# A decoder layer's products, from column-major to token-major

## The chip, the cores and the metric

The kernel runs on one core of one Trainium2 chip. The metric is the device time of one execution in microseconds (us); several executions are timed and their median is given. PE is the matrix engine, PEld its weight loads, DVE the vector engine, ACT the scalar engine, POOL GpSimd, SP the engine whose queue issues most DMAs. For a matmul the *stationary* operand (128 x up to 128) is loaded first, and the columns of the *moving* operand (up to 512) stream against it.

## The reference

One layer over 256 tokens of 2048 channels, float32. Three sub-layers, each with an RMS norm in front and a residual sum behind:

```python
h = h + 0.5 * swiglu(rms_norm(h, g1), w_gate1, w_up1, w_down1)      # 2048 -> 5632 -> 2048
proj = rms_norm(h, gm) @ w_in        # q, k, v of 16 forgetting heads, gates; q, k, v of window heads
o = concat([rms_norm(o_fox, gf), rms_norm(o_swa, gs)])
h = h + o @ w_out
h = h + 0.5 * swiglu(rms_norm(h, g2), w_gate2, w_up2, w_down2)
# swiglu(x) = (silu(x @ w_gate) * (x @ w_up)) @ w_down
```

## The kernel before

All large products are made with float32 operands cut into two parts, `hi` and `lo`, that add up to the value; of the four partial products the smallest is left out. Weights come in blocks of 1024 columns in all (512 KB): the SP queue loads `raw`, ACT copies it to `whi` (L93), DVE makes the rest `wlo` (L94). Each of these tiles has four buffers, and a block's three steps are queued with high priority, ahead of the work that stands near them in the program.

Activations are kept channel by channel: `h` holds 16 row tiles of 128 channels by 256 tokens, and `u` holds, for each row tile, the hi and lo parts side by side, 512 columns. In the feed-forward halves and the output projection (`column_major`, `columns`, L202 and L203) a 128 x 128 piece of weights is stationary: `whi` against the 512 columns of `u` (both parts), and `wlo` against the 256 columns of the hi part. The result is a 128-channel tile of [hi part | lo part] which `halves_sum` adds up (L225 on ACT, L226 on DVE). In `gated` the token's scale 1/rms, broadcast over all partitions by `rstd_rows` (L183 on PE), is multiplied in on DVE (L234), ACT takes the SiLU (L235), DVE the product (L236), and ACT and DVE cut the result into the tile `hT` (L238, L239), which the down product reads as its moving operand. `into` makes the next stage's `u` from finished rows of `h` (L150, L151) and sums squares on POOL (L163); `rstd_tokens` sums those over partitions on PE (L170).

The mixer's input projections are already made the other way round (`token_major`, `mm3`, L189 to L191): a 128 x 128 piece of `u` is stationary, and 512 (or 388) columns of weights stream, three products for each of two token tiles. The heads are then handled four at a time (`softmax_pv`): scores into PSUM tiles tagged `sc`, soft-max, PE transposes of the probabilities (L454), products with the values. PSUM's eight banks are two accumulators of two banks, two `sm` tiles and two `sc` tiles.

The output projection takes the window half first, then the forgetting half. POOL multiplies its result by the token scale and adds it to `h` (L681, L682). The first feed-forward half begins with both accumulators of its first block at once, in pieces that follow the loads of x; the last down block finishes its two column halves one after the other, so that the first store goes out earlier.

The program is unrolled. Each engine works through its own queue in order, and the order is written by a planner: among instructions whose operands its own clock takes to be ready, the one that stands earliest in the program goes first, so that later products fill gaps in the attention.

Of the kernel before, what the change touches and what calls it, by code (L numbers as in the profile page):

```python
# [17 lines left out]
P = 128  # L18
D = 2048
# [12 lines left out]
CW = 256  # L32
NCH = FF // CW
NEG = -3.0e38

# columns of the constants and of the packed vectors
# [32 lines left out]
def hybrid_layer(ctx: ExitStack, tc: tile.TileContext, a: dict, out: bass.AP):  # L69
# [6 lines left out]
    def acc_tile():  # L76
        return ps.tile([P, 2, 512], F32, tag="acc", name="acc", bufs=2)

    def small_ps(tag="sm"):
        return ps.tile([P, 512], F32, tag=tag, name=tag, bufs=2)  # L80

    # ---------------------------------------------------------------- weights
# [18 lines left out]
    h = keep.tile([P, KD, SEQ], F32, name="h")  # L101
# [63 lines left out]
    def rstd_tokens(ssq, width, tag):  # L165
        """[P, NT], the tokens' 1 / rms, from sums of squares by partition."""
# [9 lines left out]
    def rstd_rows(ssq, width, tag):  # L176
        """[P, SEQ], the same in every partition."""
        r = rstd_tokens(ssq, width, tag + "t")
        dg = sp.tile([P, NT, P], F32, tag="dg", name="dg")
        pb = small_ps()  # L180
        for t in range(NT):
            nc.vector.tensor_scalar_mul(dg[:, t, :], ident, r[:, t : t + 1])
            nc.tensor.matmul(pb[:, t * P : (t + 1) * P], lhsT=ones, rhs=dg[:, t, :], start=True, stop=True)  # L183
        rows = sp.tile([P, SEQ], F32, tag=tag, name=tag)
        nc.scalar.copy(rows, pb[:, :SEQ])
        return rows

# [5 lines left out]
    # ------------------------------------------------------- feed-forward half  # L193
    def banks(acc):
        return acc[:, 0, :], acc[:, 1, :]

    def column_major(acc, w, u, k0, k, last, cols=(0, 1)):
        """acc[j] += (128 x 256 weights).T @ parts of u; its halves' sum is the product."""
        hi, lo = w
        for j in cols:  # L200
            s = slice(k0 * CW + j * P, k0 * CW + (j + 1) * P)
            nc.tensor.matmul(acc[j], lhsT=hi[:, s], rhs=u(k), start=(k == 0), stop=False)  # L202
            nc.tensor.matmul(  # L203
                acc[j][:, 0:SEQ], lhsT=lo[:, s], rhs=u(k)[:, 0, :], start=False, stop=(k == last - 1)
            )

    def columns(acc, src, nk, u, apart=0):
        """acc = the products of nk row tiles; the columns' halves one after the other in the last ones."""
        late = []
        for b in range(nk // 4):  # L210
            with tc.high_priority():
                parts = weights(src[b])
            for k in range(4 * b, 4 * b + 4):
                if k < nk - apart:
                    column_major(acc, parts, u, k % 4, k, nk)
                else:
                    late.append((parts, k))
        for j in range(2):
            for parts, k in late:
                column_major(acc, parts, u, k % 4, k, nk, (j,))  # L220

    def halves_sum(pool, acc, tag):
        n = acc.shape[1]
        t = pool.tile([P, 2, SEQ], F32, tag=tag, name="t", bufs=1 if tag == "tu" else 2)[:, :n, :]
        nc.scalar.copy(t, acc[:, :, SEQ:])  # L225
        nc.vector.tensor_tensor(out=t, in0=acc[:, :, 0:SEQ], in1=t, op=ALU.add)  # L226
        return t

    def gated(pool, acc, rb, hT, c):
        rbb = rb.unsqueeze(1).broadcast_to([P, 2, SEQ])  # L230
        v = {}
        for nm in ("g", "u"):
            v[nm] = halves_sum(pool, acc[nm], "t" + nm)
            nc.vector.tensor_tensor(out=v[nm], in0=v[nm], in1=rbb, op=ALU.mult)  # L234
        nc.scalar.activation(v["g"], v["g"], AF.Silu)  # L235
        nc.vector.tensor_tensor(out=v["u"], in0=v["u"], in1=v["g"], op=ALU.mult)  # L236
        hs = hT[:, 2 * c : 2 * c + 2, :, :]
        nc.scalar.copy(hs[:, :, 0, :], v["u"])  # L238
        nc.vector.tensor_tensor(  # L239
            out=hs[:, :, 1, :], in0=v["u"], in1=hs[:, :, 0, :].bitcast(F32), op=ALU.subtract  # L240
        )

    def gate_up(pool, u, rb, hT, wg, wu, c0=0):
        for c in range(c0, NCH):
            acc = {}
            for nm, w in (("g", wg), ("u", wu)):
                acc[nm] = acc_tile()
                columns(banks(acc[nm]), w[c], KD, u)
            gated(pool, acc, rb, hT, c)

    def down(pool, hT, w, done, last_apart):
        for c in range(KD // 2):
            hc = h[:, 2 * c : 2 * c + 2, :]
            if not (last_apart and c == KD // 2 - 1):
                acc = acc_tile()
                columns(banks(acc), w[c], KF, tiles_of(hT))
                ends = [(acc, hc)]
            else:
                acc = [small_ps(), small_ps()]
                columns(acc, w[c], KF, tiles_of(hT), 8)  # L260
                ends = [(acc[j].unsqueeze(1), hc[:, j : j + 1, :]) for j in range(2)]
            for i, (part, hp) in enumerate(ends):
                t = halves_sum(pool, part, "tg")
                nc.vector.scalar_tensor_tensor(out=hp, in0=t, scalar=0.5, in1=hp, op0=ALU.mult, op1=ALU.add)
                done(2 * c + i, hp)

    def into(u, ssq, gcol):
        """Of two row tiles of h that are finished: the parts for u, and the squares."""

        def done(k0, hc):  # L270
            for k in (k0, k0 + 1):
                split_scaled(u(k), h[:, k, :], vec[:, gcol + k : gcol + k + 1])
            add_squares(ssq, hc, k0 == 0)

        return done

    def token_major(acc, u, nk, src_w, width=512):
        """acc[:, t, :width] = u.T @ weights, for both token tiles."""
        for kg in range(nk // 2):
            with tc.high_priority():  # L280
                hi, lo = weights(src_w[kg])
            for k in range(2):
                kk = kg * 2 + k
                m = slice(k * width, (k + 1) * width)
                for t in range(NT):
                    ts_ = slice(t * P, (t + 1) * P)
                    mm3(
                        acc[:, t, :width], u(kk)[:, 0, ts_], u(kk)[:, 1, ts_], hi[:, m], lo[:, m],
                        start=(kk == 0), stop=(kk == nk - 1),
                    )  # L290

    # ------------------------------------------------------------ first FFN
# [3 lines left out]
    with tc.tile_pool(name="f1", bufs=1) as fp:  # L296
        hT = fp.tile([P, KF, 2, SEQ], F32R, name="hT1")
        # the tensor engine's clock rises while it works: products of zeros until the first operands come
# [5 lines left out]
        take = into(u1, ss1, V_G1)  # L304
        acc = {"g": acc_tile(), "u": acc_tile()}
        tiles = {}

        def piece(nm, c):
            if c % 2 == 0:
                tiles[nm] = weight_tiles()  # L310
            at = c % 2 * 512
            weights(a["w%s1" % nm][0][c // 2][:, at : at + 512], tiles[nm], at)
            for k in range(2):
                column_major(banks(acc[nm]), tiles[nm][1:], u1, c % 2 * 2 + k, 2 * c + k, KD)

        for c in range(10):
            if c < 8:
                hc = h[:, 2 * c : 2 * c + 2, :]
                nc.sync.dma_start(hc, a["xT"][c])
                take(2 * c, hc)  # L320
                piece("g", c)
            if c >= 2:
# [441 lines left out]
```

## Time and profile before

| | |
|---|---|
| runs | 1848.87, 1857.62, 1866.74 us; median 1857.62 us |
| profiled execution | span 1855.6 us from the first to the last instruction, 26310 instructions (the page gives no other time for it) |
| PE, PEld | busy 1842.8 us (99%), 1604.5 us (86%), 10428 instructions each |
| DVE, ACT, POOL | busy 1142.0 us (62%), 895.5 us (48%), 91.1 us (5%) |
| DMA | 337.99 MB, mean 182 GB/s |
| PE's granted clock | 1.000 |

Busy time of an engine is the union of its instructions' durations. A matmul's duration includes the time in which its results travel through the array, which overlaps the next matmul; a rate is read from the distance between starts. A windows row counts each instruction that touches the window.

### The profile page before, as it was taken

Reading aid. Unit: us, or ns where it says so; the run is one execution under the profiler, and the core shown is the slowest. Engines: PE = TensorE matmul, PEld = TensorE weight load, DVE = VectorE, ACT = ScalarE, POOL = GpSimd, SP = SyncE. Lnnn points to the kernel's source line nnn. Section 1 sums busy time; section 2 is a strip of 40 time slices with the busy share of each in tenths; the row PEclk is TensorE's granted clock in tenths of the full one; section 3 lists DMA queues with packets and bytes.
Section 4 is the critical chain, followed back from the end, with each engine's and each line's share of the span. In section 5 each row is a group of like instructions: output and inputs, shape, how many; then the busy total and the mean of one; then the engine's idle time right before and its main releaser. Section 6 shows DMA issues by size and latency. Waiting matters only on the chain.

```text
span 1855.6 us, 26310 instructions
## 1 busy us (share of the span) xinstructions
PE 1842.8 (99%) x10428; PEld 1604.5 (86%) x10428; DVE 1142.0 (62%) x1394; ACT 895.5 (48%) x1182; POOL 91.1 (5%) x73
## 2 busy tenths in 40 slices
PE   8999999999999999999999999999999999999999
PEld 6888888888888888998888888888888888888887
DVE  8556665655655555658767797566666666544443
ACT  6444444444444444455766655444444444443432
POOL 2000000000000000000001462000000000000000
PEclk9999999999999999999999999999999999999999
DMA  7666555665555565565345356666665655666663
GB/s 254 190 188 187 184 190 183 187 187 184 191 184 191 185 189 185 170 203 173 115 147 159 114 161 188 188 191 193 190 186 192 193 187 190 192 189 202 191 200 114
DMA packets 97211, 337.99 MB, mean 182 GB/s; under 512 B 10816, under 2 KB 12992, under 8 KB 97088
## 3 DMA queue, kind: packets, MB, share of 16 engines
q1 hardware_dynamic: 94752, 334.10, 57.4%
q10 hardware_dynamic: 2336, 2.21, 0.3%
q8 instruction: 82, 1.34, 0.3%
q14 instruction: 41, 0.34, 0.0%
HBM read 334.17 MB, written 2.10 MB: 181 GB/s over the span
## 4 chain that ended last, share of the span: by engine, by line
PE 97%; DVE 2%; issue 1%; ACT 1%; DMA 0%; DVEq 0%
PE acc L202 53%; PE acc L203 28%; PE acc L189 4%; PE acc L191 4%; PE acc L190 4%; DVE wlo L94 1%; PE sm L202 1%; PE sm L203 1%; PE sc L558 1%; PE sm L454 1%; PE sm L460 1%; PE sc L630 1%; DVE u L151 0%; PE sm L609 0%; PE sm L461 0%
## 5 line engine op out<-in xcount | busy, mean ns | idle before, releaser
L94 DVE TENSOR_TENSOR wlo<-raw,whi 128x1024 fp32r<-128x1024 f32 (+2 forms) x648 | 794.8, 1229 | 667.8 <-ACT whi L93 667.5
L93 ACT CAST whi<-raw 128x1024 fp32r<-128x1024 f32 (+2 forms) x648 | 665.7, 1029 | 897.0 <-PE acc L202 629.6
L202 PE MATMUL acc<-u,whi 128*128 128x512 f32 x2944 | 1033.2, 395 | 1.7 <-DVE t L226 1.0
L203 PE MATMUL acc<-u,wlo 128*128 128x256 f32 x2944 | 826.9, 281 | 4.2 <-DVE wlo L94 4.2
L202 PEld LDWEIGHTS acc<-u,whi 128*128 128x128 f32 x2944 | 551.9, 188 | 132.1 <-DVE t L226 1.3
L203 PEld LDWEIGHTS acc<-u,wlo 128*128 128x128 f32 x2944 | 556.2, 189 | 7.8 <-DVE wlo L94 7.0
L202 PE MATMUL acc<-hT,whi 128*128 128x512 f32 x1320 | 463.5, 393 | 0.0
L203 PE MATMUL acc<-hT,wlo 128*128 128x256 f32 x1320 | 373.3, 283 | 0.0
L202 PEld LDWEIGHTS acc<-hT,whi 128*128 128x128 f32 x1320 | 247.9, 188 | 57.3
L203 PEld LDWEIGHTS acc<-hT,wlo 128*128 128x128 f32 x1320 | 248.2, 188 | 0.0
L189 PE MATMUL acc<-whi,u 128*128 128x512 f32 (+1 forms) x320 | 120.1, 375 | 0.6 <-ACT pr L583 0.6
L191 PE MATMUL acc<-whi,u 128*128 128x512 f32 (+1 forms) x320 | 119.4, 373 | 0.0
L190 PE MATMUL acc<-wlo,u 128*128 128x512 f32 (+1 forms) x320 | 119.4, 373 | 0.0
L226 DVE TENSOR_TENSOR t<-acc,t 128x512 f32<-128x512 f32 x119 | 81.2, 682 | 0.0
L225 ACT COPY t<-acc 128x512 f32<-128x512 f32 x119 | 68.9, 579 | 0.7 <-PE acc L203 0.7
L189 PEld LDWEIGHTS acc<-whi,u 128*128 128x128 f32 x320 | 60.1, 188 | 8.6 <-ACT pr L583 0.8
L191 PEld LDWEIGHTS acc<-whi,u 128*128 128x128 f32 x320 | 60.1, 188 | 7.9 <-issue 0.6
L190 PEld LDWEIGHTS acc<-wlo,u 128*128 128x128 f32 x320 | 60.2, 188 | 7.1
L234 DVE TENSOR_TENSOR t<-t,rb 128x512 f32<-128x512 f32 x88 | 60.7, 692 | 2.9
L202 PE MATMUL acc<-oTf,whi 128*128 128x512 f32 x128 | 45.4, 396 | 1.0 <-DVE t L226 1.0
L163 POOL TENSOR_TENSOR ssm<-ssm,sqh 128x512 f32<-128x512 f32 x7 | 9.6, 1367 | 704.8 <-ACT sqh L162 704.8
L151 DVE SCALAR_TENSOR_TENSOR u<-h,vec,u 128x256 fp32r<-128x256 f32 x48 | 40.1, 875 | 3.7 <-ACT u L150 3.7
(185 smaller groups left out, 812.6 us busy)
## 6 DMA issues: line engine op xcount, KB each, us to landing
raw<-in_wd SPq DMA_DIRECT2D x176, 512.0 KB, 3.5
raw<-in_wg SPq DMA_DIRECT2D x172, 512.0 KB, 3.5
raw<-in_wu SPq DMA_DIRECT2D x172, 512.0 KB, 3.5
raw<-in_wf SPq DMA_DIRECT2D x48, 512.0 KB, 3.9
raw<-in_wo SPq DMA_DIRECT2D x32, 512.0 KB, 3.6
raw<-in_ws SPq DMA_DIRECT2D x32, 388.0 KB, 3.1
h<-in_xT SPq DMA_DIRECT2D x8, 256.0 KB, 5.1
raw<-in_wg SPq DMA_DIRECT2D x8, 256.0 KB, 4.4
```

Source lines behind the costliest of these rows:

```text
L93: nc.scalar.copy(hi, raw)
L94: nc.vector.tensor_tensor(out=lo, in0=raw, in1=hi.bitcast(F32), op=ALU.subtract)
L151: nc.vector.scalar_tensor_tensor(out=dst[:, 1, :], in0=src, scalar=gain, in1=dst[:, 0, :].bitcast(F32), op0=ALU.mult, op1=ALU.subtract,)
L189: nc.tensor.matmul(o, lhsT=shi, rhs=mhi, start=start, stop=False)
L190: nc.tensor.matmul(o, lhsT=shi, rhs=mlo, start=False, stop=False)
L191: nc.tensor.matmul(o, lhsT=slo, rhs=mhi, start=False, stop=stop)
L202: nc.tensor.matmul(acc[j], lhsT=hi[:, s], rhs=u(k), start=(k == 0), stop=False)
L203: nc.tensor.matmul(acc[j][:, 0:SEQ], lhsT=lo[:, s], rhs=u(k)[:, 0, :], start=False, stop=(k == last - 1))
L225: nc.scalar.copy(t, acc[:, :, SEQ:])
L226: nc.vector.tensor_tensor(out=t, in0=acc[:, :, 0:SEQ], in1=t, op=ALU.add)
L234: nc.vector.tensor_tensor(out=v[nm], in0=v[nm], in1=rbb, op=ALU.mult)
L454: nc.tensor.transpose(bt[:, j * P : (j + 1) * P], src[:, j, :], ident)
```

## The change

Everything becomes token-major. `h` is kept as two token tiles by 2048 channels. In all products a 128-row by 128-token piece of `u` or `hT` is stationary and 512 columns of weights stream (`mm3`); weights are blocked by two row tiles and 512 columns instead of four and 256, the same 512 KB. The token scale becomes one value a partition: ACT takes SiLU with it straight from PSUM, and DVE multiplies the up product by it and by the SiLU in one operation. The gated block, and each finished 512-column block of `h`, are transposed on PE, eight 128 x 128 transposes a block, queued behind the second weight block of the following product (`then`). Squares are summed by ACT along the row, so POOL has no part in the norms of `h`; the residual sum is one DVE operation. The first feed-forward half starts with the gate block alone; x is loaded transposed, in chunks with two buffers, and then again by tokens into `h`. PSUM becomes six one-bank tiles `acc`, which the accumulators (two each) and the scores share, and two `sm` tiles. The output is stored by tokens.

```diff
-    def acc_tile():
-        return ps.tile([P, 2, 512], F32, tag="acc", name="acc", bufs=2)
+    def acc_pair():
+        return [ps.tile([P, 512], F32, tag="acc", name="acc", bufs=6) for _ in range(NT)]
+    def score_ps():
+        return ps.tile([P, 512], F32, tag="acc", name="sc", bufs=6)
...
-    h = keep.tile([P, KD, SEQ], F32, name="h")
+    h = keep.tile([P, NT, D], F32, name="h")
...
+    def token_major(acc, u, nk, src_w, width=512, then=(), early=None):
+        for kg in range(nk // 2):
...
+            hi, lo = parts
             for k in range(2):
                 kk = kg * 2 + k
                 m = slice(k * width, (k + 1) * width)
                 for t in range(NT):
                     ts_ = slice(t * P, (t + 1) * P)
                     mm3(
-                        acc[:, t, :width], u(kk)[:, 0, ts_], u(kk)[:, 1, ts_], hi[:, m], lo[:, m],
+                        acc[t][:, :width], u(kk)[:, 0, ts_], u(kk)[:, 1, ts_], hi[:, m], lo[:, m],
                         start=(kk == 0), stop=(kk == nk - 1),
                     )
+            if kg == 1:
+                for f in then:
+                    f()
+    def into_rows(src, c, finish):
+        for i in range(2):
+            bt = small_ps()
+            for j in range(2):
+                for t in range(NT):
+                    m = slice((2 * i + j) * P, (2 * i + j + 1) * P)
+                    nc.tensor.transpose(bt[:, j * SEQ + t * P : j * SEQ + (t + 1) * P], src[:, t, m], ident)
+            finish(4 * c + 2 * i, bt.rearrange("p (j t) -> p j t", j=2))
+    def gate_up(pool, u, rm, hT, wg, wu, first=None):
+        def split_into(k, v):
+            hs = hT[:, k : k + 2, :, :]
+            nc.scalar.copy(hs[:, :, 0, :], v)
+            nc.vector.tensor_tensor(out=hs[:, :, 1, :], in0=v, in1=hs[:, :, 0, :].bitcast(F32), op=ALU.subtract)
+        then = []
+        for b in range(FF // 512):
+            g = acc_pair()
+            if first is not None and b == 0:
+                rm = first(g)
+            else:
+                token_major(g, u, KD, wg[b], then=then)
+            s = pool.tile([P, NT, 512], F32, tag="s", name="s", bufs=1)
+            for t in range(NT):
+                nc.scalar.activation(s[:, t, :], g[t], AF.Silu, scale=rm[:, t : t + 1])
+            up = acc_pair()
+            token_major(up, u, KD, wu[b])
+            for t in range(NT):
+                nc.vector.scalar_tensor_tensor(
+                    out=s[:, t, :], in0=up[t], scalar=rm[:, t : t + 1], in1=s[:, t, :], op0=ALU.mult, op1=ALU.mult)
+            then = [lambda s=s, b=b: into_rows(s, b, split_into)]
+        return then
+    def residual(c, acc, scale):
+        for t in range(NT):
...
+            nc.vector.scalar_tensor_tensor(
+                out=h[:, t, cs], in0=acc[t], scalar=sc, in1=h[:, t, cs], op0=ALU.mult, op1=ALU.add)
+    def next_u(u, ssq, gcol, c):
...
+        for t in range(NT):
+            sq = sp.tile([P, 512], F32, tag="sqh", name="sqh", bufs=2)
+            nc.scalar.activation(sq, h[:, t, cs], AF.Square, accum_out=ssq[:, t, c : c + 1])
+        def finish(k, v):
+            for j in range(2):
+                split_scaled(u(k + j), v[:, j, :], vec[:, gcol + k + j : gcol + k + j + 1])
+        return lambda: into_rows(h[:, :, cs], c, finish)
+    def down(hT, w, then, done):
+        for c in range(D // 512):
+            acc = acc_pair()
+            token_major(acc, tiles_of(hT), KF, w[c], then=then)
+            residual(c, acc, 0.5)
+            then = done(c)
+        return then
...
+            def early(kg):
+                xc = fp.tile([P, 2, SEQ], F32, tag="xc", name="xc", bufs=2)
+                nc.sync.dma_start(xc, a["xT"][kg])
...
+            token_major(g, u1, KD, None, early=early)
+            nc.sync.dma_start(cst, a["cst"])
+            nc.sync.dma_start(pos, a["pos"])
+            for t in range(NT):
+                nc.sync.dma_start(h[:, t, :], a["x"][t])
+            return rstd_tokens(ss1, D, "r1")
...
         for half, oT, r in ((1, oTs, rs), (0, oTf, rx)):
+            for c in range(D // 512):
+                acc = acc_pair()
+                token_major(acc, oT, 8, a["wo"][half, c], then=then)
+                residual(c, acc, r)
+                then = [next_u(u2, ss2, V_G2, c)] if half == 0 else []
+        for f in then:
+            f()
```

## Rows read from the trace of the kernel before

**Rows 1.** The page: span, then busy us (share) and instructions of each engine.
```profile
span 1855.6 us, 26310 instructions
...
PE 1842.8 (99%) x10428; PEld 1604.5 (86%) x10428; DVE 1142.0 (62%) x1394; ACT 895.5 (48%) x1182; POOL 91.1 (5%) x73
```

**Rows 2.** The page: the chain that ended last, by engine.
```profile
PE 97%; DVE 2%; issue 1%; ACT 1%; DMA 0%; DVEq 0%
```

**Rows 3.** PE's lines: names, shapes, count | busy us, mean ns | idle before.
```profile
L202 PE MATMUL acc<-u,whi 128*128 128x512 f32 x2944 | 1033.2, 395 | 1.7 <-DVE t L226 1.0 <-DVE u L151 0.5
...
L202 PE MATMUL acc<-hT,whi 128*128 128x512 f32 x1320 | 463.5, 393 | 0.0
...
L202 PE MATMUL acc<-oTf,whi 128*128 128x512 f32 x128 | 45.4, 396 | 1.0 <-DVE t L226 1.0
...
L202 PE MATMUL sm<-hT,whi 128*128 128x512 f32 x88 | 30.9, 393 | 0.0
```

**Rows 4.** Windows of L202 alone, four stages: us, PE (x), PEld (x), clock, DMA.
```profile
100.00:500.00 400.00, 400.00 (x1133) 212.71 (x1132) 1.00 0.59 186
550.00:750.00 200.00, 200.00 (x571) 107.03 (x570) 1.00 0.60 185
1200.00:1550.00 350.00, 350.00 (x1011) 188.82 (x1010) 1.00 0.61 190
1600.00:1840.00 240.00, 240.00 (x685) 128.39 (x684) 1.00 0.61 191
```

**Rows 5.** PE in order of time, mixer: two rows each of 388 and 512 columns.
```profile
771.15 0.34 PE L191 MATMUL acc<-whi,u 128*128 128x388 f32 x1
...
795.00 0.34 PE L191 MATMUL acc<-whi,u 128*128 128x388 f32 x1
...
828.30 0.39 PE L191 MATMUL acc<-whi,u 128*128 128x512 f32 x1
...
849.38 0.39 PE L191 MATMUL acc<-whi,u 128*128 128x512 f32 x1
```

**Rows 6.** PE in order of time around a burst of eight transposes.
```profile
993.72 0.39 PE L191 MATMUL acc<-whi,u 128*128 128x512 f32 x1
993.96 1.03 PE L454 MATMUL sm<-cst,s 128*128 128x128 f32 x8
...
995.06 0.39 PE L190 MATMUL acc<-wlo,u 128*128 128x512 f32 x1
```

**Rows 7.** PE's lines of transposes and broadcasts; then PE in time around L170.
```profile
L454 PE MATMUL sm<-cst,s 128*128 128x128 f32 x96 | 13.6, 275 | 0.0
...
L183 PE MATMUL sm<-dg,cst 128*128 128x128 f32 x16 | 2.4, 274 | 0.0
...
767.60 0.95 PE L170 MATMUL sm<-cst,ssm 128*128 128x1 f32 x8
768.41 0.43 PE L191 MATMUL acc<-whi,u 128*128 128x388 f32 x1
```

**Rows 8.** Windows: PE, PEld, DVE, ACT, POOL busy (x), clock, DMA share, GB/s.
```profile
6.00:35.00 29.00, 25.32 (x135) 20.01 (x136) 27.60 (x45) 20.66 (x40) 10.61 (x7) 1.00 0.81 286
850.00:1050.00 200.00, 199.44 (x1097) 165.46 (x1097) 148.62 (x300) 133.07 (x282) 22.66 (x23) 1.00 0.44 140
1098.00:1128.00 30.00, 26.92 (x148) 22.24 (x146) 29.44 (x24) 16.41 (x27) 21.97 (x13) 1.00 0.52 159
```

**Rows 9.** DVE's lines from 1080 to 1125 us.
```profile
L94 DVE TENSOR_TENSOR wlo<-raw,whi 128x1024 fp32r<-128x1024 f32 x14 | 29.6, 2153 | 0.0
```

**Rows 10.** DVE's lines from 1200 to 1550 us.
```profile
L94 DVE TENSOR_TENSOR wlo<-raw,whi 128x1024 fp32r<-128x1024 f32 x127 | 155.6, 1225 | 136.2 <-ACT whi L93 136.2
...
L226 DVE TENSOR_TENSOR t<-acc,t 128x512 f32<-128x512 f32 x31 | 21.2, 683 | 0.0
```

**Rows 11.** All engines in order of time, the end.
```profile
1851.10 0.28 PE L203 MATMUL sm<-hT,wlo 128*128 128x256 f32 x1
...
1852.74 0.35 ACTq L692 DMA_DIRECT2D out<-h  x1
```

More of the change, by code (lines that the diff above doesn't have):

```diff
@@ L174, in rstd_tokens @@
         return mean_rsqrt(sp, pb[:, :NT], NT, width, tag)
[L176 to L186, printed above, removed]
     def mm3(o, shi, slo, mhi, mlo, start, stop):
@@ L191, in mm3 @@
         nc.tensor.matmul(o, lhsT=slo, rhs=mhi, start=False, stop=stop)
[L194 to L257, printed above, removed]
-            else:
[L259 to L281, printed above, removed]
+    def token_major(acc, u, nk, src_w, width=512, then=(), early=None):
+        for kg in range(nk // 2):
+            if early is not None:
+                parts = early(kg)
+            else:
+                with tc.high_priority():
+                    parts = weights(src_w[kg])
+            hi, lo = parts
@@ new lines, in residual @@
+    def residual(c, acc, scale):
+        cs = slice(c * 512, (c + 1) * 512)
+        for t in range(NT):
+            sc = scale if isinstance(scale, float) else scale[:, t : t + 1]
+            nc.vector.scalar_tensor_tensor(
+                out=h[:, t, cs], in0=acc[t], scalar=sc, in1=h[:, t, cs], op0=ALU.mult, op1=ALU.add
+            )
+    def next_u(u, ssq, gcol, c):
+        cs = slice(c * 512, (c + 1) * 512)
+        for t in range(NT):
[5 more added lines that the diff above has]
+        return lambda: into_rows(h[:, :, cs], c, finish)
@@ L293, in hybrid_layer, with rstd_blocks @@
+    def rstd_blocks(ssq, tag):
+        tot = sp.tile([P, NT], F32, tag=tag + "s", name=tag + "s")
+        nc.vector.tensor_reduce(out=tot, in_=ssq, axis=AX.X, op=ALU.add)
+        return mean_rsqrt(sp, tot, NT, D, tag)
+    def down(hT, w, then, done):
[5 more added lines that the diff above has]
+        return then
     sp = ctx.enter_context(tc.tile_pool(name="sp", bufs=1))
@@ L303, in hybrid_layer @@
             nc.tensor.matmul(warm, lhsT=zero[:, 0:P], rhs=zero, start=True, stop=True)
[L304 to L322, printed above, removed]
-                piece("u", c - 2)
-        nc.sync.dma_start(cst, a["cst"])
-        nc.sync.dma_start(pos, a["pos"])
-        rb1 = rstd_rows(ss1, D, "rb")
-        gated(fp, acc, rb1, hT, 0)
-        gate_up(fp, u1, rb1, hT, a["wg1"], a["wu1"], 1)
+        def first_block(g):
+            def early(kg):
+                xc = fp.tile([P, 2, SEQ], F32, tag="xc", name="xc", bufs=2)
+                nc.sync.dma_start(xc, a["xT"][kg])
+                tiles = weight_tiles()
+                for i in range(2):
+                    at = i * 512
+                    weights(a["wg1"][0][kg][:, at : at + 512], tiles, at)
+                for j in range(2):
+                    k = 2 * kg + j
+                    split_scaled(u1(k), xc[:, j, :], vec[:, V_G1 + k : V_G1 + k + 1])
+                add_squares(ss1, xc, kg == 0)
+                return tiles[1:]
+            token_major(g, u1, KD, None, early=early)
[4 more added lines that the diff above has]
+            return rstd_tokens(ss1, D, "r1")
@@ L329, in hybrid_layer @@
+        then = gate_up(fp, u1, None, hT, a["wg1"], a["wu1"], first_block)
         um = new_u()
-        ssm = sp.tile([P, 2, SEQ], F32, tag="ss", name="ssm")
-        down(fp, hT, a["wd1"], into(um, ssm, V_GM), False)
-    rm = rstd_tokens(ssm, D, "rm")
+        ssm = sp.tile([P, NT, 4], F32, tag="ssb", name="ssm", bufs=2)
+        then = down(hT, a["wd1"], then, lambda c: [next_u(um, ssm, V_GM, c)])
+    rm = rstd_blocks(ssm, "rm")
     with tc.tile_pool(name="mix", bufs=1) as mp:
@@ L415, in softmax_pv @@
             for jj in range(2):
-                b1 = small_ps("sc")
+                b1 = score_ps()
                 for j in range(2):
@@ L667, in hybrid_layer, with store @@
         gained(oTf, ofx, V_GF)
-        rx = rstd_rows(ssx, NH * HD, "rx")
+        rx = rstd_tokens(ssx, NH * HD, "rx")
         u2 = new_u()
-        ss2 = sp.tile([P, 2, SEQ], F32, tag="ss", name="ss2")
-        take = into(u2, ss2, V_G2)
+        ss2 = sp.tile([P, NT, 4], F32, tag="ssb", name="ss2", bufs=2)
+        then = []
         for half, oT, r in ((1, oTs, rs), (0, oTf, rx)):
-            rr = r.unsqueeze(1).broadcast_to([P, 2, SEQ])
-            for c in range(8):
-                acc = acc_tile()
-                columns(banks(acc), a["wo"][half, c], 8, oT)
-                t = halves_sum(ap_, acc, "pr")
-                hc = h[:, 2 * c : 2 * c + 2, :]
-                nc.gpsimd.tensor_tensor(out=t, in0=t, in1=rr, op=ALU.mult)
-                nc.gpsimd.tensor_tensor(out=hc, in0=hc, in1=t, op=ALU.add)
-                if half == 0:
-                    take(2 * c, hc)
-    rb2 = rstd_rows(ss2, D, "rb")
+            for c in range(D // 512):
+                acc = acc_pair()
+                token_major(acc, oT, 8, a["wo"][half, c], then=then)
[3 more added lines that the diff above has]
+            f()
+    rm2 = rstd_blocks(ss2, "rm")
     with tc.tile_pool(name="f2", bufs=1) as fp:
         hT = fp.tile([P, KF, 2, SEQ], F32R, name="hT2")
-        gate_up(fp, u2, rb2, hT, a["wg2"], a["wu2"])
-        yT = out.rearrange("(k p) t -> p k t", p=P)
-        down(fp, hT, a["wd2"], lambda k, hc: nc.scalar.dma_start(yT[:, k : k + hc.shape[1], :], hc), True)
+        then = gate_up(fp, u2, rm2, hT, a["wg2"], a["wu2"])
+        y = out.rearrange("(t p) d -> p t d", p=P)
+        def store(c):
+            cs = slice(c * 512, (c + 1) * 512)
+            for t in range(NT):
+                nc.scalar.dma_start(y[:, t, cs], h[:, t, cs])
+            return []
+        down(hT, a["wd2"], then, store)
 def _arrays(x, positions, norm_ffn1_g, ffn1_w_gate, ffn1_w_up, ffn1_w_down, norm_mix_g, w_in, b_forget,
@@ L708, in cols @@
     def cols(w):
-        return blocks(w, 4, CW)
+        return blocks(w, 2, 512)
     d["wg1"], d["wu1"], d["wd1"] = cols(ffn1_w_gate[0]), cols(ffn1_w_up[0]), cols(ffn1_w_down[0])
@@ L718, in _arrays @@
     d["xT"] = x[0].T.reshape(KD // 2, 2, P, SEQ).transpose(0, 2, 1, 3)
+    d["x"] = x[0].reshape(NT, P, D)
     d["pos"] = positions[0].reshape(NT, P).T
@@ L758 @@
     }
-    out = nc.dram_tensor("out_0", (D, SEQ), F32, kind="ExternalOutput").ap()
+    out = nc.dram_tensor("out_0", (SEQ, D), F32, kind="ExternalOutput").ap()
     with tile.TileContext(nc, schedule_with_timeline_sim=True) as tc:
```

31 lines of the change are left out of this document (17 added, 14 removed).

## The prediction

> **What bounds the kernel now.** I read the page's busy shares first: TensorE is busy 1842.8 of 1855.6 us, VectorE 62%, ScalarE 48% [rows 1]. A busy PE can hide a queue, so the chain of waits is next: 97% of what ended last is PE [rows 2]. The time is therefore the sum of PE's start-to-start intervals, and a saving elsewhere is worth nothing until PE waits for it. The windows show the one stretch where it does: from 1098 to 1128 us PE is busy 26.92 of 30 us while VectorE is busy 29.44 and GpSimd 21.97 [rows 8]. The granted clock is 1.00 in every window shown here [rows 4, 8], the 2.4 GHz level, so no step below is a clock effect. The durations of matmuls (395 ns [rows 3]) overlap and price nothing; I use starts.
>
> **The large matmuls.** The weights' cut into two parts stays, and so do the columns streamed: for 128 rows by 512 columns of weights, before, four pairs of 512 + 256 columns, 3072; after, two token tiles by three products of 512, also 3072. What falls is the count, from eight to six for the same columns. The grouped lines count the pairs: 2944 + 1320 + 88 + 128 = 4480 [rows 3], that is 1408 and 704 in each feed-forward half (gate/up, down) and 256 in the output projection. They become 1120 x 6 = 6720 matmuls.
>
> Price of a pair: the windows of L202 alone count those that touch the window, so I add 0.4 us for the one begun before it: 400.4/1133 = 353.4 ns (first gate/up), 200.4/571 = 351.0 (first down), 350.4/1011 = 346.6 (second gate/up), 240.4/685 = 351.0 (second down) [rows 4]. For the output projection, part of which is stalled, I take 346.6. Sum: 1408 x 353.4 + 704 x 351.0 + 1408 x 346.6 + 704 x 351.0 + 256 x 346.6 = 497.6 + 247.1 + 488.0 + 247.1 + 88.7 = 1568.5 us.
>
> Price of a new matmul: the mixer's projections already run that very form, token-stationary with 512 weight columns moving. Between the two L191 rows lie 31 rounds of three: (849.38 - 828.30)/93 = 226.7 ns [rows 5]. So 6720 x 226.7 = 1523.4 us, **45.1 us less**. As a check on the cause: with 388 columns 45 rounds give (795.00 - 771.15)/135 = 176.7 ns, hence 0.403 ns a column and some 20 ns fixed a matmul; 2240 fewer of them at 20 ns are also 45 us. Bounds: the first gate/up paid 6.8 ns more a pair than the second for the same form, so the form alone does not fix the price. Half of that on each matmul, 3.4 ns, is 23 us; I let it act upward as the upper end and a third of it downward (8 us), and take the value in the middle because it is the row of the very form.
>
> The Trainium skill (TensorE: Matmul & The Clock Gate, Back-to-back issue gap) puts the isolated warm gap at N/2.4 + 2.5 ns, a rule that speaks against this change: eight matmuls becoming six would save 5 ns a block, 5.6 us in all by that estimate, and the whole sum would end slower. The trace disagrees, with 226.7 ns where the rule has 215.8 and 346.6 where it has 325.
>
> **The transposes.** New on PE: a gated 512-column block needs 8 (two token tiles by four), 22 blocks; the next stage's input needs 8 for each of 4 column blocks, twice. That is 176 + 64 = 240 in 30 bursts of 8. The trace has such a burst among such matmuls: from L191 at 993.72 to the second matmul after it at 995.06 are 1.34 us, less 2 x 0.2267, 0.887 us for eight, 111 ns each [rows 6]. 240 x 0.111 = **+26.6 us**. The lower end is the same, since they sit on the bounding engine; the upper end is their duration, 275 ns [rows 7], if they did not overlap: 66 us. I take 111, a measured burst of the same length in the same surroundings.
>
> The skill's Part 4 of that page (PE-mode transpose) gives some 275 ns in one kernel's context and says that the fast clock does not engage for them; by it the burst would cost 2.2 us. The trace agrees on the duration and not on the cost or the clock: 0.887 us, at clock 1.00 from 850 to 1050 us, where nearly all of today's transposes stand.
>
> **PE work removed.** All of L183 (16 instructions, the broadcast of a token's scale over partitions) and the column sums of two norms (8 + 8 of L170) go. Eight of L170 hold PE from 767.60 to the next start at 768.41, 0.10 us each; L183 has the transposes' size and duration, so 0.11 [rows 7]. Together 16 x 0.11 + 16 x 0.10: **-3.4 us**. Below nothing and above this there is no room: they are on PE, and they go.
>
> **VectorE and GpSimd.** In gate/up, two blocks of 256 columns cost VectorE twelve operations of about 0.69 us (each block: two sums of halves, two scalings, a product, a rest) [rows 10]; one block of 512 will cost four (two scaled products, two rests). The cut of the weights, 1.23 us each, stays [rows 10]. VectorE falls, which is off the path and worth nothing there. Where it is worth something is the output projection: GpSimd's two operations a block and its sum of squares go, and beside them the cut took 2.15 us instead of 1.23 [rows 9, 10]. After, a 512 block there needs four cuts, two residual sums and four rests, 4.9 + 1.4 + about 2 = 8.3 us, under PE's 48 x 0.2267 = 10.9 us. So the 3.1 us that PE stood idle in 1098 to 1128 us [rows 8] goes: **-3.1 us**. Late next there is the last column block's chain: residual, eight transposes, rests, then the last four row tiles of the gate block; the other twelve row tiles, 72 matmuls or 16 us, can stand before it, so I cost it at nothing; without that cover it is some 4 us, once.
>
> **Start.** x is read a second time, 2.1 MB by tokens on the same SP queue as the weights, and x's transposed chunks get two buffers instead of a place each. From 6 to 35 us the DMA engines moved 286 GB/s at a share of 0.81, so 353 GB/s when full [rows 8]; 2.1 MB are 5.9 us, and the idle 19% of those 29 us is 5.5 us. Between nothing and 6 us, then; most of it fits the idle share, and I take **+2 us**. The first block's PE work is 96 x 0.2267 = 21.8 us against 64 x 0.3534 = 22.6: no term.
>
> **End.** From the start of the last matmul to the end are 1855.6 - 1851.10 = 4.5 us, of which 1.64 to the issue of the last store [rows 11]. After it: two residual sums of 512 columns, about 0.69 each, instead of copy, sum and residual of 256; and a store twice as long (128 KB more, 0.4 us at 353 GB/s): **+0.5 us**.
>
> **Sum.** -45.1 + 26.6 - 3.4 - 3.1 + 2 + 0.5 = -22.5 us against the profiled execution's 1855.6: 1833.1. The median of the runs is 2.0 us above that span, so the forecast is **1835 us**, 1.2% faster.
>
> **Rivals.**
> - The new matmuls cost more than the mixer's row: the activations of the down stage never stood as stationary operand, and equal forms differed by 6.8 ns a pair [rows 4]. At 230 ns the sum loses 22 us: 1857, no change. For it speaks that difference; against it that the mixer's interval held for 31 rounds. Chance 0.20.
> - The scores lose their own two PSUM buffers and share six with the accumulators. An output-projection pair started early holds two of them for 10.9 us; a score that waits behind two such pairs delays its unit by that much, and PE, which was busy 199.44 of 200 us there [rows 8], has less to fill in. Two units so delayed without cover are 22 us: 1857. Against it: six buffers hold three pairs, and projections fill well today. 0.12.
> - **Slower:** PE issues in order, so a burst whose input is late stops all matmuls behind it. The input is ready two VectorE products (1.4 us), and perhaps one cut (1.23), after the block's last matmul; the burst stands 24 matmuls, 5.4 us, behind that. If VectorE runs as late as in rows 8 and 9, a cover of 5.4 us can fail. It decides at 22.5/30 = 0.75 us a burst (no gain) and 1.4 us (slower by over 1%); at 2 us it gives 1895. Against: GpSimd no longer slows VectorE. 0.10.
> - Transposes cost their duration: 240 x (0.275 - 0.111) = 39 us more, 1874. This is the mechanism of the page named at the transposes. Against it stands the burst [rows 6]. 0.03.
> - A better start and steadier matmuls: below 1822. 0.05.
>
> That leaves 0.50 for the forecast's own cases, 1822 to 1848. About 1% is what a measurement of this kernel can tell from no change (its runs spread from 1848.87 to 1866.74). Faster by over 1% (below 1839): four fifths of the forecast's half, the better start, and some of the cases where a rival acts in part: 0.52. Slower by over 1% (above 1876): the in-order wait and a combination: 0.12. Within: 0.36. The range, 1816 to 1866, leaves out the slow rivals and the far low end.
>
> **What would show it.** Right: PE matmuls near 10428 - 2240 + 240 - 32 = 8396; 226 to 228 ns from start to start in all feed-forward stages; bursts of eight near 0.9 us without idle time before them; PE without idle time around the output projection; GpSimd nearly silent. Wrong: 230 ns or more between L-lines of the three products (first rival), idle PE in the mixer that ends with an accumulator's release (second), or PE waiting for VectorE just before transposes (third).

## The result, and the profile after

The changed kernel takes 1865.57 us (median of 8 runs, 1863.98 to 1866.78), the kernel before 1857.63 in the same comparison; the ratio is 1.0046, 95% interval 1.0025 to 1.0066. It is slower by half a per cent, where 1.2% faster was forecast: 30 us off in the profile's span, 1863.0 against 1833.1.

The page of the changed kernel, span and busy shares, answers to [rows 1]. The count of PE instructions is the one forecast, 8396, and PE's share is 98%, where it was 99%:

```profile
span 1863.0 us, 21805 instructions
...
PE 1834.8 (98%) x8396; PEld 1513.8 (81%) x8396; DVE 986.2 (53%) x1194; ACT 843.4 (45%) x1073; POOL 20.9 (1%) x27
```

The chain of waits is still PE's, as in [rows 2]:

```profile
PE 97%; DMA 1%; DVE 1%; ACT 0%; issue 0%; SPq 0%; DVEq 0%; ACTq 0%
```

The first of the three products (L179, one in three of the matmuls) in three stages, against [rows 4]; columns are the window, PE busy (count), PEld busy (count), clock, DMA share, GB/s:

```profile
100.00:500.00 400.00, 225.04 (x577) 108.12 (x576) 1.00 0.55 189
...
1200.00:1550.00 350.00, 196.81 (x505) 94.61 (x504) 1.00 0.55 190
1620.00:1800.00 180.00, 101.60 (x258) 48.17 (x257) 1.00 0.56 193
```

Gate/up has 577 and 505 of them. In the second window, 350.4 us less eight bursts of transposes (0.887 us each) over 3 x 505 is 226.6 ns, where 226.7 was forecast. The last row is the second down stage: 180.4/(3 x 258) = 233.1 ns, where 226.7 was forecast. In the first down stage the starts stand 233.3 ns apart.

A burst of transposes in gate/up, PE in order of time, against [rows 6]:

```profile
196.55 0.39 PE L181 MATMUL acc<-whi,u 128*128 128x512 f32 x1
196.78 1.03 PE L213 MATMUL sm<-cst,s 128*128 128x128 f32 x8
...
197.89 0.39 PE L180 MATMUL acc<-wlo,u 128*128 128x512 f32 x1
```

From the matmul ahead of it to the second behind it are again 1.34 us: 0.887 us for eight, as forecast. PE has no idle time ahead of it.

The stretch where the kernel loses most, windows with all five engines (PE, PEld, DVE, ACT, POOL busy, clock, DMA share, GB/s), and below it PE in order of time:

```profile
800.00:821.00 21.00, 21.00 (x120) 21.00 (x119) 12.37 (x14) 10.38 (x13) 0.00 (x0) 1.00 0.69 209
821.00:837.00 16.00, 1.42 (x11) 1.35 (x11) 14.05 (x41) 3.83 (x6) 0.00 (x0) 0.60 0.28 92
837.00:848.00 11.00, 9.13 (x48) 7.79 (x48) 8.16 (x20) 3.63 (x5) 0.22 (x2) 0.81 0.00 1
848.00:900.00 52.00, 52.00 (x264) 41.97 (x263) 31.93 (x65) 32.43 (x67) 1.82 (x3) 1.00 0.42 141
```

```profile
820.83 0.34 PE L181 MATMUL acc<-whi,u 128*128 128x388 f32 x1
...
821.37 0.37 PE L475 MATMUL sm<-z,cst 128*128 128x16 f32 x2
836.32 1.30 PE L532 MATMUL sm<-cst,qp 128*128 128x128 f32 x5 [14.58 <-DVE qp L524]
...
838.99 1.92 PE L546 MATMUL sc<-qk 128*128 128x128 f32 x8
...
848.39 0.58 PE L179 MATMUL acc<-whi,u 128*128 128x512 f32 x1
```

PE ends the window heads' projection at 821 us, and the next matmul of a projection starts at 848.39. In between stand 14.6 us of idle time that VectorE's product `qp` ends (the rotation of q and k), and then transposes and scores alone. The granted clock (what PE got, as a share of 2.4 GHz) is 0.60 and 0.81 on average in these stretches and 1.00 on either side. Cut finer, it is 0.50 from 836.3 to 840 us, the lower level of 1.2 GHz, and 1.00 again from 842 us, after transposes and scores. The five transposes from 836.32 take 1.30 us, where the eight of the burst above took 1.03. The Trainium skill (TensorE: Matmul & The Clock Gate, Part 1) says that an idle PE is throttled to half its clock until it has worked again; the trace agrees, with 0.50 behind 14.6 us of idle time. In the kernel before the first projection of the forgetting heads (the rows of 512 columns in [rows 5]) filled just this time.

The start and the output projection, against [rows 8], in the same columns:

```profile
6.00:35.00 29.00, 23.58 (x95) 17.22 (x96) 21.97 (x31) 20.48 (x39) 9.13 (x7) 1.00 0.93 354
...
1098.00:1128.00 30.00, 30.00 (x142) 24.81 (x141) 21.41 (x34) 17.43 (x30) 0.00 (x0) 1.00 0.50 175
```

From 1098 to 1128 us PE is busy 30.00 of 30, GpSimd silent: the stall in the output projection went as forecast. From 6 to 35 us the DMA engines are at 0.93 where they were at 0.81, and PE is busy 23.58 us instead of 25.32. That is 1.7 us less, near the 2 us forecast for the second load of x, though no run leaves that load out.

The end, all engines in order of time, against [rows 11]:

```profile
1858.21 1.39 DVE L250 SCALAR_TENSOR_TENSOR h<-acc,h 128x512 f32<-128x512 f32 x2 [8.20 <-PE acc L181]
...
1858.48 0.39 PE L181 MATMUL acc<-whi,hT 128*128 128x512 f32 x1
1858.94 1.03 ACTq L681 DMA_DIRECT2D out<-h  x2
```

From the last matmul's start to the end are 1863.0 - 1858.48 = 4.5 us, as before; the 0.5 us that I added did not come.

### The profile page after: what moved, and what is told of

It is laid out like the page before. It is cut to its first block, busy times and chain, and to the rows that moved or that the text cites. A ratio compares the mean times of both kernels' runs of the same rounds, so it can differ in the third digit from the quotient of the medians.

```text
span 1863.0 us, 21805 instructions
## 1 busy us (share of the span) xinstructions
PE 1834.8 (98%) x8396; PEld 1513.8 (81%) x8396; DVE 986.2 (53%) x1194; ACT 843.4 (45%) x1073; POOL 20.9 (1%) x27
## 4 chain that ended last, share of the span: by engine, by line
PE 97%; DMA 1%; DVE 1%; ACT 0%; issue 0%; SPq 0%; DVEq 0%; ACTq 0%
PE acc L179 31%; PE acc L181 31%; PE acc L180 31%; PE sm L213 1%; DMA xc<-in_xT 1%; PE sc L546 1%; PE sm L441 1%; PE sm L447 1%; PE sc L618 1%; PE sm L597 0%; DMA raw<-in_wg 0%; PE sm L448 0%; ACT whi L94 0%; DVE tr L516 0%; DVE qr L517 0%
## 5 line engine op out<-in xcount | busy, mean ns | idle before, releaser
L179 PE MATMUL acc<-whi,u 128*128 128x512 f32 (+1 forms) x1792 | 693.3, 388 | 2.7 <-ACT u L152 2.2
L181 PE MATMUL acc<-whi,u 128*128 128x512 f32 (+1 forms) x1792 | 691.5, 387 | 2.5 <-DVE u L153 2.5
L180 PE MATMUL acc<-wlo,u 128*128 128x512 f32 (+1 forms) x1792 | 692.0, 386 | 0.7 <-DVE wlo L95 0.7
L179 PEld LDWEIGHTS acc<-whi,u 128*128 128x128 f32 x1792 | 336.3, 188 | 69.2 <-ACT u L152 2.6
L181 PEld LDWEIGHTS acc<-whi,u 128*128 128x128 f32 x1792 | 336.2, 188 | 68.6 <-DVE u L153 3.4
L180 PEld LDWEIGHTS acc<-wlo,u 128*128 128x128 f32 x1792 | 336.5, 188 | 66.0 <-DVE wlo L95 1.9
L179 PE MATMUL acc<-whi,hT 128*128 128x512 f32 x704 | 278.5, 396 | 0.0
L180 PE MATMUL acc<-wlo,hT 128*128 128x512 f32 x704 | 278.1, 395 | 0.0
L181 PE MATMUL acc<-whi,hT 128*128 128x512 f32 x704 | 278.0, 395 | 0.0
L181 PEld LDWEIGHTS acc<-whi,hT 128*128 128x128 f32 x704 | 131.9, 187 | 32.3
L180 PEld LDWEIGHTS acc<-wlo,hT 128*128 128x128 f32 x704 | 132.0, 187 | 32.1
L179 PEld LDWEIGHTS acc<-whi,hT 128*128 128x128 f32 x704 | 132.0, 187 | 32.0
L419 ACT ACTIVATE s<-s,nm 128x128 f32<-128x128 f32 (+1 forms) x64 | 28.3, 444 | 11.2 <-DVE nm L416 8.5
L179 PE MATMUL acc<-whi,oTf 128*128 128x512 f32 x64 | 25.3, 396 | 0.0
L180 PE MATMUL acc<-wlo,oTf 128*128 128x512 f32 x64 | 25.1, 391 | 0.0
L181 PE MATMUL acc<-whi,oTf 128*128 128x512 f32 x64 | 25.0, 391 | 0.0
```

The source lines that it names most:

```text
L179: nc.tensor.matmul(o, lhsT=shi, rhs=mhi, start=start, stop=False)
L180: nc.tensor.matmul(o, lhsT=shi, rhs=mlo, start=False, stop=False)
L181: nc.tensor.matmul(o, lhsT=slo, rhs=mhi, start=False, stop=stop)
L419: nc.scalar.activation(s[:, j, :], s[:, j, :], AF.Exp, bias=nm[:, i, j : j + 1], accum_out=den[:, i, j : j + 1],)
```

## The experiments

| kernel | time, us | ratio to before, 95% interval |
|---|---|---|
| before (the comparisons' medians) | 1849.05 to 1858.22 | |
| changed | 1865.57 | 1.0046 (1.0025 to 1.0066) |
| own_scores | 1846.11 | 0.9945 (0.9917 to 0.9973) |
| fox_first | 1853.85 | 0.9977 (0.9950 to 1.0003) |
| hT_aligned | 1852.74 | 0.9992 (0.9964 to 1.0020) |
| down_from_u | 1858.47 (one run) | |
| both | 1832.96 | 0.9899 (0.9877 to 0.9921) |
| hT_at_256 | 1847.00 (one run) | |
| no_transposes | 1813.13 | 0.9792 (0.9765 to 0.9819) |
| before_hT_128 | 1842.85 | 0.9949 (0.9931 to 0.9967) |
| u_off, all_off | 1865.38, 1830.92 (one run each) | |

The median of the kernel before moves between comparisons because its runs stand at three levels (last experiment); times of one table row are compared with each other first.

### own_scores: the scores get their own PSUM tiles

```diff
-        return [ps.tile([P, 512], F32, tag="acc", name="acc", bufs=6) for _ in range(NT)]
+        return [ps.tile([P, 512], F32, tag="acc", name="acc", bufs=4) for _ in range(NT)]
-        return ps.tile([P, 512], F32, tag="acc", name="sc", bufs=6)
+        return ps.tile([P, 512], F32, tag="sc", name="sc", bufs=2)
```

> The changed kernel with PSUM split as before: four one-bank tiles for the accumulators, two of their own for the scores. Theory (the six shared tiles go to the six score tiles of the first two window units, which stand earlier in the program, so the first forgetting-head projection finds no accumulator and PE has nothing to do while VectorE rotates q and k): the 14.6 us of idle PE that ends at 836 us and the half-clock stretch behind it go, no PE gap over 1.5 us after the first 50 us, 17 to 21 us less, 1845 to 1849 us. Rival (VectorE's rotation is late for any order, since the planner puts the transposes of q there): the idle stretch stays, 1863 to 1867 us.

1846.11 us, 19.5 less. The same two windows as above, and PE's lines between 821 and 848 us (count | busy us, mean ns | idle):

```profile
821.00:837.00 16.00, 16.00 (x75) 13.40 (x75) 13.54 (x27) 9.24 (x11) 0.00 (x0) 1.00 0.63 198
837.00:848.00 11.00, 11.00 (x50) 9.10 (x49) 10.86 (x25) 5.02 (x6) 0.00 (x0) 1.00 0.54 187
```

```profile
L179 PE MATMUL acc<-whi,u 128*128 128x512 f32 x39 | 15.3, 392 | 0.0
L181 PE MATMUL acc<-whi,u 128*128 128x512 f32 x38 | 14.8, 389 | 0.0
L180 PE MATMUL acc<-wlo,u 128*128 128x512 f32 x38 | 14.8, 389 | 0.0
```

115 matmuls of the projection now stand where PE idled, at clock 1.00. The gain is the one that the theory named, and the rival is out.

### fox_first: the order instead of the tiles

```diff
+        fox_qk(0)
         window_unit(0)
         window_unit(1)
-        fox_qk(0)
```

> The changed kernel with the six PSUM tiles still shared, but the first forgetting-head projection (q and k of half 0) written ahead of the first two window units. Theory (tiles are given out in program order): the projection gets its accumulators and covers the rotation, the idle stretch at 821 to 836 us goes as with separate tiles, 1844 to 1850 us. Rival (sharing as such costs, by scores and accumulators waiting for each other all through the mixer): less than half of the stall's 19 us comes back, 1855 us or more.

1853.85 us: 11.7 of the 19.5 us come back, between the two bands. The first window shows that the stall at 821 us is gone with all six tiles still shared. The second, and PE's waits (us, times, longest), show new idle time later in the mixer, ahead of the transposes of the forgetting heads:

```profile
800.00:850.00 50.00, 50.00 (x253) 45.01 (x252) 38.85 (x67) 26.00 (x32) 0.00 (x0) 1.00 0.64 202
850.00:900.00 50.00, 43.94 (x239) 36.08 (x238) 38.06 (x101) 31.68 (x82) 0.56 (x5) 0.93 0.25 84
```

```profile
PE sm L597 <- issue: 5.6, 2, 4.1
...
PE sm L597 <- DVE qa L585: 1.9, 1, 1.9
```

So the place in the program decides who gets the shared tiles: window units 0 and 1 ask for three score tiles each, six in all, and whoever comes after them waits. The changed kernel's trace fits: all 32 score instructions of these two units (L546) stand between 836 us and the projection's first matmul at 848.39. Moving the projection mends that place and opens others. What those 5.6 us of "issue" wait for the profile does not say.

### hT_aligned: hT 32 bytes further on

```diff
     sp = ctx.enter_context(tc.tile_pool(name="sp", bufs=1))
+    sp.tile([P, 8], F32, name="pad")
```

> The changed kernel with 32 bytes a partition more ahead of hT, so that hT starts at a multiple of 64 bytes like u (in the changed kernel it starts 32 bytes past one). Theory (the down stage's 233.4 ns from start to start against gate/up's 226.7 come from where hT starts): the down stages fall to 226 to 228 ns, 2112 x 6.7 ns = 14 us less, 1850 to 1853 us. Rival (the operand's place in memory has no part in it; it is its contents or the stage): 233 ns stays, 1863 to 1867 us.

1852.74 us, 12.8 less. L179 in the second gate/up and the second down stage:

```profile
1200.00:1550.00 350.00, 196.78 (x504) 94.62 (x504) 1.00 0.57 189
1620.00:1800.00 180.00, 102.92 (x265) 49.74 (x265) 1.00 0.61 202
```

265 in 180 us instead of 258: 180.4/(3 x 265) = 226.9 ns. The theory holds, though its "multiple of 64" does not (below).

The pad moves whatever is placed behind it, too, and with it `oTf`, the stationary operand of one half of the output projection (192 matmuls). In the changed kernel their starts stand 229 ns apart, here from the first of these rows to the second, 15 matmuls on:

```profile
1093.54 0.39 PE L180 MATMUL acc<-wlo,oTf 128*128 128x512 f32 x1
...
1096.98 0.39 PE L180 MATMUL acc<-wlo,oTf 128*128 128x512 f32 x1
```

With the pad they stand 233.3 ns apart, some 0.8 us more in all, so the 12.8 us are the down stages' gain less this loss.

### down_from_u: another operand in the same stage

```diff
-        down(hT, a["wd2"], then, store)
+        down(hT, a["wd2"], then, store, lambda k: u2(k % KD))
```

> The changed kernel, but the second half's down product reads the 16 row tiles of u in turn as its stationary operand instead of the 44 of hT (hT is made and not used). If the 233.4 ns belong to the operand hT (its place or its contents): the second down stage falls to 226 to 228 ns while the first stays at 233, 1056 x 6.7 ns = 7 us less, about 1858 us. If they belong to the stage (44 row tiles into one accumulator, its weights, its neighbours): both stay at 233 ns and the time at 1865 us.

1858.47 us, 7.1 less in one run. L179 in the first and the second down stage:

```profile
550.00:750.00 200.00, 111.63 (x283) 52.86 (x282) 1.00 0.55 183
...
1620.00:1800.00 180.00, 103.08 (x265) 49.62 (x265) 1.00 0.61 201
```

The second has 265 in its 180 us, 226.9 ns; the first keeps 283 in 200 us, which is 236 ns with its bursts of transposes counted in and 233 without. It is the operand, not the stage.

### both

The two mends together (the diffs of own_scores and hT_aligned).

> The changed kernel with both mends: scores in PSUM tiles of their own, and hT 32 bytes further on. If the two causes are independent, the two gains measured alone add: 1865.6 - 19.5 - 12.8 = 1833 us, 1830 to 1837, which is the prediction's sum (1833.1 us in the profile's span). If they overlap (the same wait counted twice), 1840 us or more.

1832.96 us in six runs, ratio 0.9899 (0.9877 to 0.9921); the span is 1831.3 where the prediction's sum had 1833.1. The two causes add. It is faster than the kernel before, too.

### hT_at_256, u_off, all_off: which place counts

By the addresses that the program gives its tiles, u, the weights' parts and hT start 64 bytes short of a multiple of 256 in the kernel with both mends. In hT_at_256 the pad ahead of hT is 96 bytes; in u_off u is moved, with a second pad behind it; in all_off all three.

```diff
-    sp.tile([P, 8], F32, name="pad")
+    sp.tile([P, 24], F32, name="pad")     # hT_at_256
...
     h = keep.tile([P, NT, D], F32, name="h")
+    keep.tile([P, 16], F32, name="pad64")     # u_off, all_off
...
     u1 = new_u()
+    keep.tile([P, 48], F32, name="pad192")     # u_off
```

> As the kernel with both mends, but hT starts at a multiple of 256 bytes, where u, the weights and hT there start 64 bytes short of one. If a start at a multiple of 64 bytes is what counts, the down stages stay at 226 to 228 ns and the time at 1831 to 1838 us. If stationary operand and moving weights must start alike, the down stages go back above 229 ns, and the time to 1840 us or more.

> As the kernel with both mends, but u is moved by 64 bytes to a multiple of 256, while hT and the weights' parts keep their place 64 short of one. If what counts is that stationary operand and moving weights start at the same place modulo 256 bytes, gate/up goes from 226.9 to about 233.3 ns, 4224 x 6.5 = 27 us more (and some 5 us in the mixer and the output projection), 1860 to 1867 us, while the down stages keep 227. If it was something about hT alone, gate/up keeps 227 and the time 1833.

> As the kernel with both mends, but u, the weights' parts and hT are all moved by 64 bytes, to multiples of 256. If only their place relative to each other counts, all stages keep 226 to 228 ns and the time 1831 to 1836 us. If the place 64 short of a multiple of 256 is itself the good one, all stages go to about 233 ns, 6720 x 6.5 = 44 us more, 1877 us.

1847.00, 1865.38 and 1830.92 us, one run each. The first product (L179, in the last two kernels L180) in the second gate/up and the second down stage, first hT_at_256, then u_off, then all_off:

```profile
1200.00:1550.00 350.00, 197.04 (x506) 94.85 (x506) 1.00 0.57 190
1620.00:1800.00 180.00, 101.71 (x258) 48.32 (x257) 1.00 0.60 197
```

```profile
1200.00:1550.00 350.00, 193.87 (x491) 91.72 (x490) 1.00 0.55 185
1620.00:1800.00 180.00, 102.71 (x264) 49.38 (x263) 1.00 0.59 198
```

```profile
1200.00:1550.00 350.00, 196.75 (x504) 94.73 (x505) 1.00 0.57 190
1620.00:1800.00 180.00, 102.89 (x266) 49.76 (x265) 1.00 0.61 202
```

hT_at_256: 258 in the down stage, 233 ns, though hT starts at a multiple of 64 and of 256. u_off: the slow stage changes over, gate/up has 491 where it had 505, and down 264. all_off: 504 and 266, both fast. So no place is good by itself: what counts is where the stationary operand starts relative to the moving weights. At the same place modulo 256 bytes the rate was the fast one in all these runs. Slow, at 233 ns, were a stationary operand 32 bytes before that place (hT in the changed kernel, oTf with both mends) and 64 bytes past it (hT in hT_at_256, u in u_off). 64 bytes before it, oTf in the changed kernel took 229 ns, so the price depends on the distance and its side. All operands that were fast start alike modulo 512 as well; whether 256 would do no run shows, nor why the place counts.

### before_hT_128: the same in the kernel before

```diff
     sp = ctx.enter_context(tc.tile_pool(name="sp", bufs=1))
+    sp.tile([P, 32], F32, name="pad")
```

> The kernel before with 128 bytes more ahead of hT: there hT is the moving operand and starts at a multiple of 64 bytes already, but 64 past a multiple of 256, while u starts 192 past one. If only the multiple of 64 counts: a pair in the down stages keeps its 351 ns, and the time 1857 us. If hT must start like u: 346.6 ns, 1408 x 4.4 ns = 6 us less, about 1851 us.

1842.85 us, 6.2 less than the median of the kernel before in that comparison, and 5.7 less than its fastest run. L202 in three stages:

```profile
100.00:500.00 400.00, 400.00 (x1155) 215.75 (x1155) 1.00 0.62 190
...
1200.00:1550.00 350.00, 350.00 (x1011) 189.29 (x1010) 1.00 0.62 190
1620.00:1800.00 180.00, 180.00 (x520) 97.32 (x520) 1.00 0.64 199
```

The down stage now has 520 in 180.4 us, 346.9 ns a pair instead of 351; the gate/up stages stand at 400.4/1155 = 346.7 and 350.4/1011 = 346.6. The second expectation holds, so the place counts for column-major pairs as well: 128 bytes apart is slow, and alike is fast.

### no_transposes: what the transposes cost

hT is cut from the product as it stands, by tokens, so the values that the down products read are others:

```diff
-            then = [lambda s=s, b=b: into_rows(s, b, split_into)]
+            def untransposed(s=s, b=b):
+                for i in range(2):
+                    split_into(4 * b + 2 * i, s[:, i, :].rearrange("p (j t) -> p j t", j=2))
+            then = [untransposed]
```

> As the kernel with both mends, without the 176 transposes of the gated blocks: hT is cut from the untransposed product, so the down products read other numbers. Theory (a transpose on the bounding engine costs its start-to-start distance, 111 ns, and nothing waits for it): 176 x 0.111 = 19.5 us less than the kernel with both mends. Rival (each costs its duration of 272 ns): 48 us less. Rival (bursts stop PE for their input): over 25 us less, and with both mends PE shows idle time ahead of transposes.

1813.13 us, 19.8 less than both: 113 ns each of the 176, against 111 forecast. The Trainium skill (TensorE: Matmul & The Clock Gate, Part 4: PE-mode transpose) gives some 275 ns for a transpose in one kernel's context. The trace agrees on the duration (272 ns here), but that is not what a transpose costs among these matmuls. L179 in the two gate/up stages without bursts:

```profile
100.00:500.00 400.00, 228.83 (x589) 110.36 (x588) 1.00 0.59 193
...
1200.00:1550.00 350.00, 200.13 (x516) 96.66 (x515) 1.00 0.59 194
```

400.4/(3 x 589) = 226.6 ns and 350.4/(3 x 516) = 226.4: the matmuls beside them keep their price.

### before_again and before_third: the levels of the kernel before

The kernel before, unchanged.

> The kernel before, unchanged, for a second profile: its runs stand at 1848.7, 1857.7 and 1866.7 us and nowhere between. If each of the two gate/up stages runs a pair at either 346.7 or 353.3 ns in an execution (1408 x 6.6 = 9.3 us each), the profile's gate/up stages show those two values alone, and the span follows from which: about 1846.5 us with both short, 1855.6 with one, 1864.5 with both long. If the levels come from elsewhere, span and pairs do not go together.

> The kernel before once more, for a third profile; the same expectation as for the second: the span is 1846.5 us plus 9.3 for each gate/up stage whose pairs take 353.3 ns.

1857.68 and 1857.63 us, both with a span of 1855.6. L202 in before_again (before_third has the same counts):

```profile
100.00:500.00 400.00, 400.00 (x1155) 215.79 (x1154) 1.00 0.62 190
...
1200.00:1550.00 350.00, 350.00 (x991) 186.09 (x991) 1.00 0.60 186
1620.00:1800.00 180.00, 180.00 (x513) 96.26 (x513) 1.00 0.64 197
```

Now the first gate/up has 1155 in 400.4 us, 346.7 ns a pair, and the second 991 in 350.4, 353.6: the other way round than in [rows 4], at the same span. So a gate/up stage takes one of two values in an execution, whichever stage it is. Executions with both short or both long were not profiled; that the levels 1848.7 and 1866.7 are those rests on their distance, 9.0 us, against 1408 x 6.6 ns = 9.3. The kernel with hT moved by 128 bytes, where nothing else is changed, stood at 1842.73 to 1843.19 in all its ten runs. What sets the value stays open.

## Why the prediction was wrong

**The price of a new matmul** is the first step that failed: I took 226.7 ns from the mixer's row for all 6720. It holds for 4416 of them. For the 2112 whose stationary operand is hT it is 233.3: 2112 x 6.6 ns = 13.9 us (measured by hT_aligned: 12.8, with 0.8 us lost at oTf). The other 192, with oTf, took 229, another 0.4 us. My first rival named the operand, one that had never stood as stationary, and priced it at 22 us for all matmuls; that the operand's place was the reason it did not say. I read the 351 ns of the down pairs as noise of the form. They were an effect of the same kind: hT's start, 128 bytes off (before_hT_128). The rows that hinted at it were in my own group [rows 4], both down stages at 351.0 while gate/up varied.

**The PSUM tiles had no term in the sum.** The second rival named the sharing, but the wrong victim: scores waiting behind accumulators. It was the accumulators of the next projection that waited behind scores, so that the filler and not the attention went missing. My sign for it, idle time that ends with an accumulator's release, did not come: the idle time ended with `qp`. That my price, 22 us, is near the 19.5 that own_scores gave back is luck. Behind the idle time PE ran at the lower clock until 842 us, where I had written that no step is a clock effect. I had looked for the cover in PE's busy share (199.44 of 200 us from 850 on), and the stall stands just ahead of that window, at 821 to 848, where the rows of 512 columns show the projection running as cover.

**The chances.** I treated the rivals as exclusive. They act on different stages, and both happened: 13.9 + 19.5 = 33 us on a gain of 22.5. With 0.20 and 0.12 for each alone, a range that let them add would have reached 1880; mine was drawn for one of them alone, 1857, and some more, up to 1866. It holds the 1865.57 by 0.4 us, and that is luck: with the two causes' measured sizes my sum makes some 1868. What came out against the forecast is the direction.

**What was right.** The sum without the two: 1833.1 us against 1831.3 in both. The transposes (26.6 us; 113 ns each measured), the output projection's stall (3.1 us, gone), the start (2 us against 1.7 less busy time, not tested by itself), the in-order wait ahead of the bursts (none). The end was 0.5 us over, and with the two causes added to the forecast (1833.1 + 13.9 + 19.5 = 1866.5) some 3 us are over in all, which I cannot place: the mends give 31.7 us together, 33.2 alone in spans.

**What the change itself is worth.** Like against like, each with its hT placed well, token-major is 1832.96 and column-major 1842.85, 9.9 us apart. In terms: pairs at 346.6 cost 4480 x 346.6 = 1552.8 us, the new matmuls 1523.4, so 29 us less; less the transposes' 26.6, and the 6 us of removed work and stall, and 2 at the start, makes 7. A third of the 45 us that I booked was the misplaced hT and the long gate/up stage of the kernel before, not its form.

## What to carry to other kernels

Before one row prices an operand that it does not contain, look whether equal forms with other operands have the same distance between starts; where they differ steadily by stage, the place of the operands is a suspect, and a few bytes of padding the test. When tiles of two uses share one set of buffers, go through the program's order and count who takes them at each turn: here they were given out in that order, and what loses them may be the work that covers somebody else's wait. Rivals that act in different stages add up; give their joint case a chance.

## What the hardware showed that I had not expected

- A 128 x 512 float32r matmul goes from 226.7 to 233.3 ns from start to start when its stationary operand starts 32 bytes before the moving one's place modulo 256 or 64 past it, and to 229 ns when 64 before; a column-major pair goes from 346.7 to 351 ns at 128 bytes.
- A gate/up stage of column-major pairs runs whole at 346.7 or at 353.3 ns a pair, with the same program, and the two stages can change roles from one execution to the next.
- A burst of eight transposes among these matmuls took the same 0.887 us in the changed kernel's gate/up as in the mixer of the kernel before, at clock 1.00; leaving 176 out gave 113 ns each.
